# The order of twelve matmuls in a token-major weight unit: low weights first, and two PSUM banks in turn

## Chip, cores and metric

The kernel runs on one core of a Trainium2 chip. The metric is the device time of one execution in microseconds (us). The kernel before takes 2206.59 us, the median of three runs (2205.45 to 2206.94). One profiled execution gives the trace that this document reads.

## What is computed

One layer of a decoder on 256 tokens with 16 learned tokens put ahead of them, in float32, with a model width of 2048:

```python
h = concat([meta, x])                                  # 16 + 256 tokens
h = h + 0.5 * swiglu(rmsnorm(h), w_gate, w_up, w_down) # 2048 -> 5632 -> 2048
h = h + mixer(rmsnorm(h), w_in, ...)                   # two attentions, sigmoid gates, w_out
h = h + 0.5 * swiglu(rmsnorm(h), w_gate, w_up, w_down)
return h[:, 16:]
# swiglu(x) = (silu(x @ w_gate) * (x @ w_up)) @ w_down
# mixer: proj = x @ w_in gives q, k, v of 8 + 8 heads and two gates;
#        (sigmoid(g_fox) * (o_fox @ w_fox) + sigmoid(g_sb) * (o_sb @ w_sb)) @ w_out
```

Nearly all the work is the products of these activations with weight matrices of 394 MB in all (from their shapes).

## The kernel before

**Products from two parts.** TensorE multiplies in a float32 form of reduced precision, so each operand is split into a high part (the value rounded to that form) and a low part (the rest). A product is the sum of three matmuls: high by high, high by low and low by high, all summed up in one PSUM bank.

**Units and blocks.** A block is one tile of columns of a weight matrix, mostly 512 wide, with its whole contraction. It is worked through in units of 1024 columns' worth of weights per partition, which for 512 columns are two k-tiles of 128 rows. For each unit SyncE loads the raw weights (`load`), ScalarE rounds them to the high weights `wh` (L190, or L1130 in a group, see below), VectorE subtracts to get the low weights `wl` (L191 or L1136), and TensorE multiplies (`products`). There are three buffers each of `wh` and `wl` (`SPLIT_BUFS`), and a unit is split two units ahead of its products (`ahead`).

Units come in four kinds:

- feature-major units with 272 tokens (24 matmuls of 272 columns, L1204): the first feed-forward layer, keys and values;
- "wide" units with 256 tokens (L1187, L1190): queries and the output projection;
- **token-major units** (`by_token`): here the activations are the stationary operand, 128 tokens by 128 features, and the weights stream by, 512 columns. Each block has two halves of 128 tokens, and each half has a bank of its own. A unit has 2 k-tiles x 2 halves x 3 terms = 12 matmuls. 216 units in 44 blocks are of this kind: the gates (64 units), the two branch projections (32), the first two column groups of the second feed-forward layer (32) and its down projection (88). That is 2592 of the program's 13716 matmuls;
- **group units** (class `Group`, L1003): column groups 2 to 10 of the second feed-forward layer are done with seven products p1 to p7 of half size instead of eight. A group has 28 units with 6 matmuls of 512 columns each, all into one bank. Some of them read weight sums formed earlier, and the units of p2 cost VectorE one more subtraction (L1135).

In the second feed-forward layer the group units and the token-major units (second column group first, then the down projection) are interleaved: a token-major unit follows each unit of p2, every second unit of p5 and p3, and one unit each of p1 and p7, as long as there are any; the last 14 follow at the end.

**A token-major unit before.** L1181 loops over the halves j, and inside it L1192 over the k-tiles i. For each (j, i) come high activations by high weights, high activations by low weights, low activations by high weights (L1195 to L1204). So the six matmuls of half 0 come first, then the six of half 1. After each half, if the block ends there, its bank is emptied (`b.evac`, for the down projection `down2`, L933), and `tick()` is called twice.

**Lanes.** `tick()` advances small side jobs written as generators: the attention of the heads, the sigmoids of the gates, and the transposes of finished activations (`turn`, L440). A job yields the number of ticks until its next step. A group unit ticks once, a token-major unit four times.

**Order.** The program text gives each instruction a place. The order in which each engine really runs them is fixed when the program is built, by a planner with its own estimates of durations: an instruction whose inputs are not due yet by those estimates may be passed by a later one on the same engine. Matmuls into the same bank stay in the order of the text. On the chip each engine then runs its list in order.

Of the kernel before, what the change touches and what calls it, by code (L numbers as in the profile page):

```python
# [16 lines left out]
P = 128  # L17
# [35 lines left out]
def hybrid_layer(ctx: ExitStack, tc: tile.TileContext, x, meta_tokens, ffn1_norm, ffn1_w_gate, ffn1_w_up,  # L53
# [3 lines left out]
    act, dve, pe = nc.scalar, nc.vector, nc.tensor  # L57
# [21 lines left out]
    def name(tag):  # L79
        uid[0] += 1  # L80
        return f"{tag}_{uid[0]}"
# [4 lines left out]
    def temp(shape, dt, tag, bufs=1):  # L86
        return tp.tile(shape, dt, tag=tag, name=name(tag), bufs=bufs)
# [14 lines left out]
    def tick():  # L102
        for k, lane in lanes.items():
            if waits[k]:
                waits[k] -= 1
            while lane and not waits[k]:
                try:
                    waits[k] = next(lane[0]) or 1
                except StopIteration:
                    lane.pop(0)  # L110
# [863 lines left out]
    class Group:  # L974
# [18 lines left out]
        def products(self, p, u, wh, wl):  # L993
            k = self.BANK[p]
            if k not in self.banks:
                self.banks[k] = psp.tile([P, 512], F32, tag="ps", name=name("acc"))
            ps = self.banks[k]
            fresh = p in ("p1", "p2", "p4", "p5")
            xh, xl = forms[self.FORM[p]]
            for i in range(2):  # L1000
                kt = 2 * u + i
                for m, (a, b) in enumerate(((xh, wh), (xh, wl), (xl, wh))):
                    pe.matmul(ps[:], a[:, kt, :], b[:, i, :], start=fresh and kt == 0 and m == 0,  # L1003
                              stop=kt == 7 and m == 2, skip_group_check=True)
            if u == 3:
                getattr(self, p)(ps)
# [97 lines left out]
    raws, halves, banks, newest = {}, {}, {}, []  # L1104
# [63 lines left out]
    def products(u):  # L1168
        b, k0, n = units[u]
        wh, wl = halves.pop(u)  # L1170
        if isinstance(b, Group):
            b.products(k0, n, wh, wl)
            tick()
            return
        outs = 2 if b.by_token else b.cols // P
        if k0 == 0:
            if b.before:
                b.before()
            banks[b] = [psp.tile([P, 512], F32, tag="ps", name=name("acc")) for _ in range(outs)]
        wide = not b.by_token and b.n == NR  # L1180
        for j in range(outs):  # L1181
            ps = banks[b][j]
            cs = slice(j * P, (j + 1) * P)
            if wide:
                xs_of = [b.rhs(k0 + i) for i in range(n)]
                for i, x in enumerate(xs_of):
                    pe.matmul(ps[:].rearrange("p (a t) -> p a t", a=2), wh[:, i, cs], x[:, :, :NR],  # L1187
                              start=k0 + i == 0, stop=False, skip_group_check=True)
                for i, x in enumerate(xs_of):
                    pe.matmul(ps[:, :NR], wl[:, i, cs], x[:, 0, :NR], start=False, stop=k0 + i == b.kts - 1,  # L1190
                              skip_group_check=True)
            for i in range(0 if wide else n):  # L1192
                x = b.rhs(k0 + i)
                first, last = k0 + i == 0, k0 + i == b.kts - 1
                if b.by_token:  # L1195
                    xh, xl = (x[0][j], x[1][j]) if isinstance(x, list) else (x[:, 0, cs], x[:, 1, cs])
                    terms = ((ps[:], xh, wh[:, i, :]), (ps[:], xh, wl[:, i, :]), (ps[:], xl, wh[:, i, :]))
                elif b.stacked:
                    terms = tuple((ps[:, :b.n], wh[:, i, cs], x[:, m, :b.n]) for m in range(2))
                else:  # L1200
                    o, xh, xl = ps[:, :b.n], x[:, 0, :b.n], x[:, 1, :b.n]
                    terms = ((o, wh[:, i, cs], xh), (o, wh[:, i, cs], xl), (o, wl[:, i, cs], xh))
                for m, (o, a, c) in enumerate(terms):
                    pe.matmul(o, a, c, start=first and m == 0, stop=last and m == len(terms) - 1)  # L1204
            if wide and k0 + n == b.kts:
                t = temp([P, NR], F32, "sum", bufs=3)
                act.activation(t[:], ps[:, NR:2 * NR], AF.Copy)
                dve.tensor_tensor(t[:], t[:], ps[:, :NR], op=ALU.add)
                ps = t
            if k0 + n == b.kts:  # L1210
                if b is blocks[0]:
                    held.append((b.evac, j, ps))
                else:
                    b.evac(j, ps)
            for _ in range(2 if b.by_token else 1):
                tick()
        if k0 + n == b.kts:
            del banks[b]
# [42 lines left out]
    with tc.manual_schedule(engines={act.engine, dve.engine}):  # L1261
        act.preload_act_table_set(LN_EXP)
        first_start()
        first_products(0)
        first_norm(1)
        first_products(1)
        raws.pop(0)
        halves.pop(0)
        for u in range(1, KT // 2 - 1):
            first_norm(u + 1)  # L1270
            if u == KT // 2 - 3:
                lanes["misc"] += [first_factors(), first_block(), other_constants()]
            products(u)
    done = KT // 2
    start = KT // 2 - 1
    for u in range(start, len(units)):
        ahead(u)
        products(u)
# [33 lines left out]
```

## Time and profile before

| | |
|---|---|
| median of three runs | 2206.59 us (2205.45 to 2206.94) |
| the profiled execution's own time | 2207.63 us |
| its span, first to last instruction | 2205.9 us |
| granted TensorE clock, mean | 0.999 |
| TensorE busy, matmuls | 2199.1 us, 13716 instructions |
| VectorE busy | 1603.0 us |
| ScalarE busy | 1170.5 us |
| memory traffic | 250 GB/s over the span |

Rows of the groups view have: line, engine, operation, output tile <- input tiles, shape, count | busy us, mean ns of one | idle time of the engine before them, and what ended it. In this kernel `v` and `f` are buffers of activations (and of other values), `acc` is a PSUM bank of a block, `aux` one of a side job. So `acc<-wh,v` with 512 columns is a token-major matmul with high weights. Rows of the timeline have: start us, duration us, engine, line, operation, tiles, shape and how many in a row were merged; in brackets the idle time before and what ended it. PE is the matmul, PEld the load of the stationary operand, which runs ahead of its matmul. The ends of matmuls are modelled (a 512-column one always shows 0.39 us or more), so the step from one start to the next is the measure of what one costs. A start can likewise be shown early where the load of its stationary operand came late.

### The profile page before, as it was taken

Reading aid. Unit: us, or ns where it says so; the run is one execution under the profiler, and the core shown is the slowest. Engines: PE = TensorE matmul, PEld = TensorE weight load, DVE = VectorE, ACT = ScalarE, POOL = GpSimd, SP = SyncE. Lnnn points to the kernel's source line nnn. Section 1 sums busy time; section 2 is a strip of 40 time slices with the busy share of each in tenths; the row PEclk is TensorE's granted clock in tenths of the full one; section 3 lists DMA queues with packets and bytes.
Section 4 is the critical chain, followed back from the end, with each engine's and each line's share of the span. In section 5 each row is a group of like instructions: output and inputs, shape, how many; then the busy total and the mean of one; then the engine's idle time right before and its main releaser. Section 6 shows DMA issues by size and latency. Waiting matters only on the chain.

```text
span 2205.9 us, 34841 instructions
## 1 busy us (share of the span) xinstructions
PE 2199.1 (100%) x13716; PEld 1997.0 (91%) x13716; DVE 1603.0 (73%) x1944; ACT 1170.5 (53%) x1467; POOL 42.1 (2%) x113
## 2 busy tenths in 40 slices
PE   9999999999999999999999999999999999999999
PEld 9999999999999999998899988888888888888887
DVE  6676666667766765889556665667888888888886
ACT  6344433334443454656445565458666666666663
POOL 0000000000000001110000000000000000000000
PEclk9999999999999999999999999999999999999999
DMA  7899999999999966555655456555788777888774
GB/s 225 281 330 324 340 318 348 343 338 333 347 336 340 323 202 191 164 166 158 190 183 164 146 156 201 179 187 163 241 272 269 261 262 260 275 272 270 258 260 171
DMA packets 262021, 554.09 MB, mean 251 GB/s; under 512 B 17289, under 2 KB 22241, under 8 KB 261857
## 3 DMA queue, kind: packets, MB, share of 16 engines
q1 hardware_dynamic: 259776, 548.34, 75.2%
q8 instruction: 107, 1.75, 0.3%
q10 hardware_dynamic: 1472, 2.37, 0.3%
q0 software_dynamic: 608, 1.16, 0.2%
q14 instruction: 58, 0.47, 0.1%
HBM read 493.07 MB, written 58.73 MB: 250 GB/s over the span
## 4 chain that ended last, share of the span: by engine, by line
PE 99%; DMA 0%; DVE 0%; SPq 0%; issue 0%; DVEq 0%; ACT 0%
PE acc L1204 72%; PE acc L1003 16%; PE acc L1187 5%; PE acc L1190 3%; PE aux L727 1%; PE aux L600 1%; PE aux L440 1%; PE aux L588 0%; PE aux L698 0%; DMA v<-in_meta_tokens_dram 0%; PE acc L1165 0%; PE aux L866 0%; PE aux L340 0%; PE aux L677 0%; PE aux L678 0%; PE aux L640 0%
## 5 line engine op out<-in xcount | busy, mean ns | idle before, releaser
L190 ACT ACTIVATE wh<-raw 128x1024 fp32r<-128x1024 f32 (+1 forms) x609 | 644.4, 1059 | 779.1 <-PE acc L1204 621.9
L191 DVE TENSOR_TENSOR wl<-raw,wh 128x1024 fp32r<-128x1024 f32 (+1 forms) x609 | 743.1, 1222 | 432.3 <-ACT wh L190 428.3
L1204 PE MATMUL acc<-v,wh 128*128 128x272 f32 x5264 | 991.4, 288 | 0.0
L1204 PEld LDWEIGHTS acc<-v,wh 128*128 128x128 f32 x5264 | 827.4, 189 | 0.1
L1204 PE MATMUL acc<-v,wl 128*128 128x272 f32 x2616 | 753.5, 289 | 0.4 <-DVE wl L191 0.4
L1204 PE MATMUL acc<-wh,v 128*128 128x512 f32 x1664 | 540.8, 392 | 0.0
L1204 PEld LDWEIGHTS acc<-v,wl 128*128 128x128 f32 x2616 | 490.8, 188 | 0.8 <-DVE wl L191 0.6
L1204 PEld LDWEIGHTS acc<-wh,v 128*128 128x128 f32 x1664 | 312.5, 188 | 64.6
L1136 DVE TENSOR_TENSOR wl<-raw,wh 128x1024 fp32r<-128x1024 f32 x252 | 305.1, 1221 | 41.5 <-ACT wh L1130 33.4
L1130 ACT ACTIVATE wh<-raw 128x1024 fp32r<-128x1024 f32 x252 | 266.5, 1060 | 124.3 <-PE acc L1204 75.4
L1204 PE MATMUL acc<-wl,v 128*128 128x512 f32 x832 | 327.8, 394 | 0.0
L1204 PEld LDWEIGHTS acc<-wl,v 128*128 128x128 f32 x832 | 156.2, 188 | 38.8 <-DVE wl L191 7.1
L1003 PE MATMUL acc<-wh,f 128*128 128x512 f32 x576 | 191.3, 393 | 0.0
L1187 PE MATMUL acc<-v,wh 128*128 128x512 f32 x512 | 160.6, 395 | 0.0
L1003 PE MATMUL acc<-wh,v 128*128 128x512 f32 x432 | 143.3, 389 | 0.0
L1003 PEld LDWEIGHTS acc<-wh,f 128*128 128x128 f32 x576 | 108.2, 188 | 22.5
L1190 PEld LDWEIGHTS acc<-v,wl 128*128 128x128 f32 x512 | 96.1, 188 | 22.0
L1003 PE MATMUL acc<-wl,f 128*128 128x512 f32 x288 | 113.2, 393 | 0.0
L1190 PE MATMUL acc<-v,wl 128*128 128x256 f32 x512 | 101.3, 279 | 0.0
L1003 PEld LDWEIGHTS acc<-wh,v 128*128 128x128 f32 x432 | 81.1, 188 | 16.9
L1003 PE MATMUL acc<-wl,v 128*128 128x512 f32 x216 | 84.0, 389 | 0.0
L1187 PEld LDWEIGHTS acc<-v,wh 128*128 128x128 f32 x512 | 78.4, 188 | 0.2
(264 smaller groups left out, 1378.5 us busy)
## 6 DMA issues: line engine op xcount, KB each, us to landing
raw<-in_ffn_w_down_dram SPq DMA_DIRECT2D x176, 512.0 KB, 5.4
raw<-in_ffn_w_gate_dram SPq DMA_DIRECT2D x175, 512.0 KB, 5.2
raw<-in_w_in_dram SPq DMA_DIRECT2D x162, 512.0 KB, 3.7
raw<-in_ffn_w_up_dram SPq DMA_DIRECT2D x140, 512.0 KB, 5.1
sum<-pre SPq DMA_DIRECT2D x108, 512.0 KB, 6.5
raw<-sum SPq DMA_DIRECT2D x108, 512.0 KB, 4.6
pre<-in_ffn_w_up_dram SPq DMA_DIRECT2D x72, 512.0 KB, 6.9
pre<-in_ffn_w_gate_dram SPq DMA_DIRECT2D x36, 512.0 KB, 6.8
```

The lines of the kernel that those rows point to most:

```text
L190: act.activation(hi, src, AF.Copy)
L191: dve.tensor_tensor(lo, src, hi.bitcast(F32), op=ALU.subtract)
L440: pe.transpose(p[:, (2 * j + i) * P:(2 * j + i + 1) * P], u[:, i, c:c + P], ident[:])
L600: pe.matmul(po[:, :NR], a[:, ks], b[:, i * NR:(i + 1) * NR], start=n == 0, stop=n == 6)
L727: pe.matmul(o, a, b, start=start, stop=stop, skip_group_check=True)
L1003: pe.matmul(ps[:], a[:, kt, :], b[:, i, :], start=fresh and kt == 0 and m == 0, stop=kt == 7 and m == 2, skip_group_check=True)
L1130: act.activation(wh[:], raw[:], AF.Copy)
L1136: dve.tensor_tensor(wl[:], raw[:], wh[:].bitcast(F32), op=ALU.subtract)
L1187: pe.matmul(ps[:].rearrange("p (a t) -> p a t", a=2), wh[:, i, cs], x[:, :, :NR], start=k0 + i == 0, stop=False, skip_group_check=True)
L1190: pe.matmul(ps[:, :NR], wl[:, i, cs], x[:, 0, :NR], start=False, stop=k0 + i == b.kts - 1, skip_group_check=True)
L1204: pe.matmul(o, a, c, start=first and m == 0, stop=last and m == len(terms) - 1)
```

## The change

In a token-major unit all twelve matmuls are now issued ahead of the loop over halves. For each of the two k-tiles i they are: high activations by **low** weights for half 0 and half 1, then high activations by high weights for both halves, then low activations by high weights for both. So successive matmuls go to the two banks in turn, and the first two of a unit read the low weights. The emptying of the banks and the ticks stay in the loop over halves, with the same order among themselves, and so come behind all twelve. Number, shapes and operands of the matmuls are the same; in each bank the order of the three terms differs.

```diff
+        if b.by_token:
+            todo = [(i, l, m, j) for i in range(n) for l, m in ((1, 0), (0, 0), (0, 1)) for j in range(outs)]
+            for i, l, m, j in todo:
+                x = b.rhs(k0 + i)
+                a = x[m][j] if isinstance(x, list) else x[:, m, j * P:(j + 1) * P]
+                pe.matmul(banks[b][j][:], a, (wh, wl)[l][:, i, :], start=k0 + i + m == 0 and l == 1,
+                          stop=k0 + i == b.kts - 1 and m == 1)
         for j in range(outs):
             ps = banks[b][j]
...
-            for i in range(0 if wide else n):
+            for i in range(0 if wide or b.by_token else n):
                 x = b.rhs(k0 + i)
                 first, last = k0 + i == 0, k0 + i == b.kts - 1
-                if b.by_token:
-                    xh, xl = (x[0][j], x[1][j]) if isinstance(x, list) else (x[:, 0, cs], x[:, 1, cs])
-                    terms = ((ps[:], xh, wh[:, i, :]), (ps[:], xh, wl[:, i, :]), (ps[:], xl, wh[:, i, :]))
-                elif b.stacked:
+                if b.stacked:
                     terms = tuple((ps[:, :b.n], wh[:, i, cs], x[:, m, :b.n]) for m in range(2))
```

## The prediction

> **What bounds the kernel now.** I read the page first: the busy times and the chain that ended last; then who TensorE's loads waited for; then the timeline at those places.
>
> ```profile
> span 2205.9 us, 34841 instructions
> PE 2199.1 (100%) x13716; PEld 1997.0 (91%) x13716; DVE 1603.0 (73%) x1944; ACT 1170.5 (53%) x1467; POOL 42.1 (2%) x113
> PE 99%; DMA 0%; DVE 0%; SPq 0%; issue 0%; DVEq 0%; ACT 0%
> ...
> PEld acc L1204 <- DVE wl L191: 9.4, 29, 0.6
> PEld acc L1003 <- DVE wl L1136: 1.3, 7, 0.2
> ```
>
> TensorE is the chain from end to end. A change of order can move the end in two ways only: through the step from one matmul to the next, or through idle time of TensorE. The only waits that recur in the steady part are those of the last two rows, and both are for low weights. That is what the change touches: it makes a unit ask for its low weights with its first matmul, not its second.
>
> **The step.** Near the end of the trace there are token-major units alone, with nothing late:
>
> ```profile
> 2200.17 0.39 PE L1204 MATMUL acc<-wl,v 128*128 128x512 f32 x1
> 2200.39 0.62 PE L1204 MATMUL acc<-wh,v 128*128 128x512 f32 x2
> ...
> 2200.82 0.75 DVE L933 SCALAR_TENSOR_TENSOR v<-acc,v 128x256 f32<-128x256 f32 x2 [3.23 <-PE acc L1204]
> ...
> 2201.76 0.39 PE L1204 MATMUL acc<-wh,v 128*128 128x512 f32 x1
> ...
> 2202.18 0.76 DVE L933 SCALAR_TENSOR_TENSOR v<-acc,v 128x256 f32<-128x256 f32 x2 [0.60 <-PE acc L1204]
> ...
> L933 DVE SCALAR_TENSOR_TENSOR v<-acc,v x50: 414/682/692, 1708.2 to 2202.5; 128x512 f32<-128x512 f32 x46, 128x256 f32<-128x256 f32 x4
> ```
>
> The last row gives one piece of the emptying by itself (shortest, median, longest in ns). From 2200.17 to 2201.76 are seven steps: 0.227 us each, in one bank but for one. Does a change of bank make it shorter? The side jobs have a place where two banks take turns (L640 and L641) and others of the same widths in one bank:
>
> ```profile
> 969.84 0.29 PE L640 MATMUL aux<-kqh,onesr 128*128 128x272 f32 x1
> ...
> 970.33 0.39 PE L1204 MATMUL acc<-wh,v 128*128 128x512 f32 x1
> ...
> 974.47 0.40 PE L600 MATMUL aux<-R,vh 128*128 128x256 f32 x2
> ...
> 975.30 0.40 PE L1204 MATMUL acc<-wh,v 128*128 128x512 f32 x1
> ...
> 1040.71 0.29 PE L677 MATMUL aux<-kqh 128*128 128x272 f32 x1
> ...
> 1041.08 0.40 PE L1204 MATMUL acc<-wh,v 128*128 128x512 f32 x1
> ```
>
> In turn: two of 272 and two of 256 columns take 0.49 us. In one bank: seven of 256 take 0.83 (0.119 each), three of 272 take 0.37 (0.123 each), so two and two would take 0.484. The turn gains nothing that the trace can tell. The same number of matmuls at the same step: 0.
>
> **Where low weights are late.** Three kinds of place, all in the interleaved part of the second feed-forward layer. Kind A, at 1744:
>
> ```profile
> 1743.03 1.05 ACT L1130 ACTIVATE wh<-raw 128x1024 fp32r<-128x1024 f32 x1
> 1743.17 1.23 DVE L191 TENSOR_TENSOR wl<-raw,wh 128x1024 fp32r<-128x1024 f32 x1 [0.57 <-ACT wh L190]
> ...
> 1744.11 0.39 PE L1204 MATMUL acc<-wh,v 128*128 128x512 f32 x1
> 1744.45 0.50 PE L1204 MATMUL acc<-wl,v 128*128 128x512 f32 x1
> 1744.79 0.64 PE L1204 MATMUL acc<-wh,v 128*128 128x512 f32 x2
> ```
>
> The unit starts at 1744.11, its low weights are finished at 1744.40. The next matmul but one starts at 1744.79, so the one with low weights really ran from 1744.79 - 0.227 = 1744.56: 0.17 after the end of the subtraction, 0.45 after the unit's start. Of that, 0.227 is covered by the first matmul; TensorE idles 0.23. Kind B, at 1763:
>
> ```profile
> 1763.44 0.62 PE L1204 MATMUL acc<-wh,v 128*128 128x512 f32 x2
> 1763.89 0.27 PE L440 MATMUL aux<-ident,v 128*128 128x128 f32 x1
> 1763.92 0.48 PE L1003 MATMUL acc<-wh,f 128*128 128x512 f32 x1
> 1764.26 0.50 PE L1204 MATMUL acc<-wl,v 128*128 128x512 f32 x1
> 1764.60 0.62 PE L1204 MATMUL acc<-wh,v 128*128 128x512 f32 x2
> ```
>
> Here the planner knew that the low weights would be late and filled: the first matmul of half 0, the first of half 1 (another bank, so it may pass), a transpose, the first matmul of the next group unit. The low weights could be used from 1764.60 - 0.227 = 1764.37, 0.93 after the start. Kind C, at 1990:
>
> ```profile
> 1987.45 1.28 DVE L933 SCALAR_TENSOR_TENSOR v<-acc,v 128x512 f32<-128x512 f32 x2
> 1988.65 1.21 DVE L1135 TENSOR_TENSOR raw<-raw,raw 128x1024 f32<-128x1024 f32 x1
> ...
> 1990.23 0.61 PE L1003 MATMUL acc<-wh,f 128*128 128x512 f32 x2
> 1990.68 0.62 PE L1204 MATMUL acc<-wh,v 128*128 128x512 f32 x2
> ...
> 1990.92 1.22 DVE L191 TENSOR_TENSOR wl<-raw,wh 128x1024 fp32r<-128x1024 f32 x1
> 1991.13 0.42 PE L1003 MATMUL acc<-wl,f 128*128 128x512 f32 x1
> 1991.39 0.62 PE L1003 MATMUL acc<-wh,f 128*128 128x512 f32 x2
> ...
> 1992.31 0.40 PE L1204 MATMUL acc<-wl,v 128*128 128x512 f32 x1
> ```
>
> Now a **group** unit lacks its low weights, and the two leading matmuls of the next token-major unit, which need high weights alone, are put in front of it. They fill 0.45 us; the group unit's low weights are usable from 1991.39 - 0.227 = 1991.16, 0.03 after that.
>
> The count comes from the two rows of waits: 7 of L1003 are kind C (first at 1668, last at 2125). Of the 29 of L1204, following the timeline, one is in a feature-major unit at 320 and one in a token-major unit at 1542; 8 are kind B (1629 to 2099) and 19 kind A (1571 to 2147). One more filled place without a wait is at 1561.
>
> **The change, costed.** Low weights first means that a token-major unit has nothing to offer before they are there: both banks begin with them, and in a bank the order holds. Those leading high matmuls were the cover.
>
> - Kind C: the group unit's low weights come when they came (1991.16), the two matmuls in front of it are gone: 0.45 us idle at each, 7 x 0.45 = 3.2. After that follow five group matmuls to 1992.30, and the token-major low weights (finished 1990.92 + 1.22 = 1992.14, plus 0.17) are there at 1992.31: nothing further.
> - Kind B: of four fills the transpose and the group matmul stay; 0.45 us each goes. 8 x 0.45 = 3.6; at best, with three more transposes of 0.11 put in, 8 x 0.12 = 1.0.
> - Kind A: 0.227 us of cover goes; without a fill 19 x 0.227 = 4.3. With the fill it is nothing: the high weights of the next group unit are finished at 1743.03 + 1.05 = 1744.08, before 1744.11, and its first matmul needs only them. Will the planner put it there? In kind B it still filled at 0.56 and no longer at 0.79, while the chip had the weights at 0.93: its estimates run 0.14 to 0.37 early. In kind A the chip has them at 0.45, so the planner expects them at 0.08 to 0.31 after the start, and then it fills. I take 0; end for the range 4.3.
> - The single places at 1542 and 1561: 0.23 and 0.45, together 0.7.
> - Other token-major units of that part, 56 of them, stand as the one at 1749:
>
> ```profile
> 1748.41 1.23 DVE L191 TENSOR_TENSOR wl<-raw,wh 128x1024 fp32r<-128x1024 f32 x1 [0.40 <-ACT wh L190]
> ...
> 1749.84 0.39 PE L1204 MATMUL acc<-wh,v 128*128 128x512 f32 x1
> ```
>
> Finished at 1749.64, usable at 1749.81, start at 1749.84: on time by 0.03. I take 0; with 0.05 each it would be 2.8. This margin is tight but it is tied: the high weights wait for the buffer of the unit three back, whose last reader is in both orders a unit's twelfth matmul. The low buffer comes free at the eighth instead of the eleventh, but the subtraction waits for the high weights anyway: no gain. In the gates, the branches and at the end no row of waits names a token-major unit: 0.
>
> - Emptying: half 0 was emptied under the six matmuls of half 1; now both halves come together, at the end. Down-projection rows show 1.28 us for two. The next block writes other banks of the eight, so TensorE doesn't wait; VectorE does both (0.6 apart) in the 1.3 us before the next high weights are rounded. At kind C VectorE goes from the emptying at 1987.45 without a gap to the late low weights, and half 0's would now wait for the unit's end at about 1987.7: 0.26 each if nothing is put in front, 7 x 0.26 = 1.8. I take 0, since the subtraction of L1135, next in its list, needs no matmul.
> - The very end has no such cover (one piece takes 0.42, two 0.76): the last matmul is at 2201.76, VectorE starts 0.42 later at 2202.18. Now half 0's two pieces begin at 2201.53 + 0.42 = 2201.95 and take two steps of 0.34, so half 1's begin at 2202.63: +0.45.
> - Ticks: four at the end of a unit, where there were two and two. The number and what they issue are the same; a job that feeds TensorE yields 4 to 7 ticks before it goes on, at least one unit of 2.7 us, and what isn't due the planner passes. 0, at most 1.
>
> Sum: 3.2 + 3.6 + 0 + 0.7 + 0.45 = **7.9 us**. Against the profiled execution's 2207.63 that is 2215.5; the profiled execution is 1.0 above the median, so I forecast 2206.6 + 7.9 = **2214.5 us**.
>
> **Rivals.**
> 1. *The cover only moves (no change).* The planner finds other fills at B and C as it did with the transpose: then B costs its lower bound 1.0, C half of its 3.2, and with the single places and the end it is 1.0 + 1.6 + 0.7 + 0.45 = 3.7: 2210.3. For it: it does fill. Against: at C the next unit's high weights aren't ready yet and nothing else is in sight. 0.28.
> 2. *Faster: the turn of banks shortens the step.* The place is the 2592 token-major matmuls; each ns is worth 2.6 us, and from 1.7 ns the kernel is measurably faster. If the step fell to 0.220, the time would be 2206.6 + 7.9 - 18 = 2196. Against it are the rows of the turn above; for it only that 0.227 is more than 512 columns need at the rate of the steps between 256 and 512 (0.227 - 0.119 = 0.108 per 256), a fixed 0.011 that has some cause. 0.12.
>    The Trainium skill, "TensorE: Matmul & The Clock Gate", section "Wait — 56ns, not 53.3ns?", gives 215.7 ns from start to start at 512 columns; the trace shows 227, and by the page's figure 29 us would lie in these units if the bank were the cause. The page doesn't say so.
> 3. *Slower than forecast.* No fill at A (4.3), VectorE's late emptying (1.8), the tight 56 (2.8): up to +17, 2223. For it: the planner left A unfilled before. 0.1.
> 4. *Much slower: each block loses an overlap.* If emptying half 0 under half 1 was cover everywhere, each of the 44 blocks loses the 0.6 us of one half: 26 us more, 2233 from the median alone. Against it: the emptying at 1987.45 ran on while TensorE went on to a group unit in another bank. 0.02.
>    The Trainium skill has such a rule, which speaks against this change: in "Perfetto Trace Analysis", section Matmuls, independent matmul groups should rotate through different banks so that emptying one overlaps the next one's matmuls. By that rule the 26 us would stand; the trace bears it out for the last block only.
> 5. *The change does nothing,* because the planner restores the old order. It can't: within a bank the text holds. Under 0.01.
>
> **How the numbers follow.** Forecast 0.48 with a range of its own of 2211 to 2219; rivals 0.28, 0.12, 0.1, 0.02 and next to nothing. A difference under 0.2% (4.4 us: 2202.2 to 2211.0) can't be told from no change in this kernel. Slower: forecast and rivals 3 and 4, 0.6. No change: rival 1, 0.28. Faster: 0.12. The range 2204 to 2221 takes in rival 1 and the upper ends of most terms.
>
> **What will show it.** Right: the waits of L1204's successor for `wl` of L191 grow from 9.4 us, those of the group line from 1.3 us by some 3; at kind C no token-major pair stands in the group unit; at kind A a group matmul stands ahead of the first low one; the token-major step is still 0.227. Wrong: a step of 0.225 or less; waits unchanged (then planner fills); or new waits of ScalarE or side jobs, which I cost at nothing.

## The result, and the profile after

| | before | after |
|---|---|---|
| median | 2206.66 us (five runs, 2205.45 to 2207.09) | 2219.88 us (five runs, 2219.06 to 2222.62) |
| ratio | 1 | 1.0063, 95% interval 1.0052 to 1.0075 |
| the profiled execution: its time, its span | 2207.63, 2205.9 us | 2221.49, 2219.8 us |
| last matmul's start to the end of the span | 4.17 us | 4.70 us |

The change makes the kernel slower by 13.2 us between the medians, 0.60% (the ratio in the table is that of the means). The forecast was 7.9 us, so the direction was right and the size too small: the median lies 0.9 us above the forecast's own range of 2211 to 2219 and inside the wide one of 2204 to 2221. In the kernel after, L1186 is the token-major line (L1204 before); L1003 is still the group line.

Three rows of the page of the kernel after, then its waits of TensorE's loads (us in total, times, longest):

```profile
span 2219.8 us, 34842 instructions
PE 2207.2 (99%) x13716; PEld 1994.6 (90%) x13716; DVE 1603.1 (72%) x1944; ACT 1168.3 (53%) x1467; POOL 41.4 (2%) x113
PE 96%; ACT 2%; DVE 2%; issue 1%; DMA 0%; SPq 0%; DVEq 0%; ACTq 0%
...
PEld acc L1186 <- DVE wl L191: 11.5, 27, 0.7
PEld acc L1003 <- ACT wh L1130: 7.3, 23, 0.8
PEld acc L1003 <- DVE wl L1136: 5.6, 9, 0.8
```

The same matmuls, but the chain that ended last now leaves TensorE for 3 to 4% of the span, to the two engines that make the weights. The second row of waits is new: group loads that wait for **high** weights. All 23 are group matmuls that the planner pulls forward: 19 at kind A, three at kind B, one at 1561. Most of this wait is the load's alone; the table below counts what it costs the matmuls.

Where is it? Busy time by stage of the kernel after (window | its length, PE busy and instructions, PEld, DVE, ...):

```profile
960.00:1558.00 598.00, 597.75 (x3378) 523.48 (x3377) 402.11 (x568) 336.80 (x467) 17.22 (x49) 1.00 0.57 174
1700.00:1900.00 200.00, 198.76 (x866) 158.84 (x867) 167.44 (x157) 127.14 (x134) 0.00 (x0) 1.00 0.79 260
1900.00:2166.00 266.00, 263.54 (x1148) 209.82 (x1147) 225.67 (x214) 171.43 (x181) 0.00 (x0) 1.00 0.78 260
```

And of the kernel before:

```profile
960.00:1558.00 598.00, 597.92 (x3377) 523.39 (x3376) 401.87 (x568) 338.47 (x467) 18.12 (x49) 1.00 0.57 174
1700.00:1900.00 200.00, 200.00 (x884) 162.75 (x883) 171.41 (x163) 131.38 (x138) 0.00 (x0) 1.00 0.80 267
1900.00:2166.00 266.00, 266.00 (x1176) 216.39 (x1176) 231.14 (x221) 174.02 (x183) 0.00 (x0) 1.00 0.80 266
```

In the gates, attention and branches nothing changes: 3378 matmuls against 3377. In the last of these windows TensorE starts 1148 instructions instead of 1176, at 0.227 us some 6 us less work in the same time. The granted clock is 1.00 in all. So all of the loss lies where group units and token-major units alternate.

To place it there, each step from one matmul's start to the next was compared with its nominal one (0.227 us at 512 columns, 0.108 for a transpose) and the excess added up. From 1558 to 2166 that is 7.3 us before and 20.6 after, +13.3. With +0.53 behind the last matmul this is 13.8, and the spans differ by 13.9. By kind of place:

| place | count | before, us | after, us | difference | predicted |
|---|---|---|---|---|---|
| C, in a group unit | 7 | 0.1 | 4.2 (0.60 each) | +4.1 | +3.2 |
| B | 8 | 1.1 (0.14 each) | 4.6 (0.49, three times 0.71) | +3.4 | +3.6 |
| A | 19 | 4.2 (0.22 each) | 5.0 (0.16 to 0.33, once 0.70) | +0.8 | 0 |
| D, the next token-major unit after a kind A | 18 | 0 | 3.4 (0.19 each) | **+3.4** | **0** |
| the place at 1561 | 1 | 0 | 0.4 | +0.4 | +0.45 |
| steps with under 0.08 too much | many | 1.9 | 3.1 | +1.2 | 0 |

A step counts as such a place from 0.08 us of excess; smaller ones, such as the 0.03 at six of the seven kind C places before, stand in the last row. The place at 1542 gives another 0.3, and between 1250 and 1450 the excess is 0.4 smaller, without a kind of place that repeats.

**Kind C, in the kernel after.** The timeline at 2000:

```profile
1999.21 1.22 DVE L1136 TENSOR_TENSOR wl<-raw,wh 128x1024 fp32r<-128x1024 f32 x1
...
1999.54 0.61 PE L1003 MATMUL acc<-wh,f 128*128 128x512 f32 x2
...
2000.48 0.50 PE L1003 MATMUL acc<-wl,f 128*128 128x512 f32 x1 [0.33 <-DVE wl L1136]
...
2000.81 0.62 PE L1003 MATMUL acc<-wh,f 128*128 128x512 f32 x2
```

No token-major pair stands in front of the late matmul. It is due at 1999.54 + 2 x 0.227 = 1999.99 and really runs from 2000.81 - 0.227 = 2000.58, 0.59 late. (The bracket says 0.33, because the ends of matmuls are modelled and this start is shown early.)

**Kind B,** at 1767:

```profile
1766.65 1.22 DVE L191 TENSOR_TENSOR wl<-raw,wh 128x1024 fp32r<-128x1024 f32 x1
1766.87 0.39 PE L1003 MATMUL acc<-wh,f 128*128 128x512 f32 x1
...
1767.10 0.27 PE L440 MATMUL aux<-ident,v 128*128 128x128 f32 x1
...
1767.13 0.48 PE L1003 MATMUL acc<-wh,f 128*128 128x512 f32 x1
...
1767.45 0.27 PE L440 MATMUL aux<-ident,v 128*128 128x128 f32 x1
...
1768.48 1.09 PE L1186 MATMUL acc<-wh,v 128*128 128x512 f32 x4
```

The unit's turn comes at 1766.87 + 0.227 = 1767.10. The low weights can be used from 1768.48 - 2 x 0.227 = 1768.03, 0.93 later, exactly as before. The transpose and the group matmul still fill, one more transpose was found (0.11), and the 0.45 of the two high matmuls is gone: 0.48 idle.

**Kinds A and D,** the same kind of unit at 1747 and the next one at 1753:

```profile
1746.65 1.23 DVE L191 TENSOR_TENSOR wl<-raw,wh 128x1024 fp32r<-128x1024 f32 x1 [0.57 <-ACT wh L190]
...
1747.36 0.75 PE L1003 MATMUL acc<-wh,v 128*128 128x512 f32 x2
...
1747.95 0.71 PE L1186 MATMUL acc<-wl,v 128*128 128x512 f32 x2
...
1748.50 0.85 PE L1186 MATMUL acc<-wh,v 128*128 128x512 f32 x3
...
1750.97 1.06 ACT L190 ACTIVATE wh<-raw 128x1024 fp32r<-128x1024 f32 x1 [2.12 <-PE acc L1186]
...
1752.07 1.22 DVE L191 TENSOR_TENSOR wl<-raw,wh 128x1024 fp32r<-128x1024 f32 x1
...
1753.04 0.39 PE L1003 MATMUL acc<-wh,v 128*128 128x512 f32 x1
...
1753.35 0.73 PE L1186 MATMUL acc<-wl,v 128*128 128x512 f32 x2
...
1753.92 0.62 PE L1186 MATMUL acc<-wh,v 128*128 128x512 f32 x2
```

At A the planner does what was predicted: the second of the two matmuls shown at 1747.36 belongs to the next group unit. It takes the place of the high matmul, and the idle time stays at 0.2. But then the unit at 1753 is late. Its subtraction starts at 1752.07 and its turn comes at 1753.04 + 0.227 = 1753.27: 1.20 us. In the prediction's rows of 1748 the subtraction starts at 1748.41 and the turn comes at 1749.84: 1.43 us. The missing 0.23 is one matmul. The rounding of those weights (1750.97) starts when the unit of kind A has ended and its buffer is free; up to the next token-major unit there used to be twelve group matmuls, and one of the twelve has been used up as the fill. The margin of 0.03 of the "56 tight units" becomes 0.19 too little at each of these 18.

### The profile page after: what moved, and what is told of

Its sections match the earlier page's. It is cut to its first block, busy times and chain, and to the rows that moved or that the text cites. A ratio compares the mean times of both kernels' runs of the same rounds, so it can differ in the third digit from the quotient of the medians.

```text
span 2219.8 us, 34842 instructions
## 1 busy us (share of the span) xinstructions
PE 2207.2 (99%) x13716; PEld 1994.6 (90%) x13716; DVE 1603.1 (72%) x1944; ACT 1168.3 (53%) x1467; POOL 41.4 (2%) x113
## 4 chain that ended last, share of the span: by engine, by line
PE 96%; ACT 2%; DVE 2%; issue 1%; DMA 0%; SPq 0%; DVEq 0%; ACTq 0%
PE acc L1208 45%; PE acc L1186 26%; PE acc L1003 14%; PE acc L1194 5%; PE acc L1197 3%; PE aux L727 1%; PE aux L600 1%; PE aux L440 1%; DVE wl L1136 0%; DVE wl L191 0%; ACT wh L1130 0%; ACT wh L190 0%; ACT v L878 0%; DMA v<-in_meta_tokens_dram 0%; DVE v L1033 0%
## 5 line engine op out<-in xcount | busy, mean ns | idle before, releaser
L1186 PE MATMUL acc<-wh,v 128*128 128x512 f32 x1664 | 456.0, 391 | 0.0
L1186 PEld LDWEIGHTS acc<-wh,v 128*128 128x128 f32 x1664 | 312.3, 188 | 68.9
L1136 DVE TENSOR_TENSOR wl<-raw,wh 128x1024 fp32r<-128x1024 f32 x252 | 305.1, 1222 | 47.5 <-ACT wh L1130 41.8
L1186 PE MATMUL acc<-wl,v 128*128 128x512 f32 x832 | 266.1, 398 | 2.1 <-DVE wl L191 2.1
L1003 PE MATMUL acc<-wh,f 128*128 128x512 f32 x576 | 190.4, 395 | 0.0
L1186 PEld LDWEIGHTS acc<-wl,v 128*128 128x128 f32 x832 | 149.4, 188 | 39.6 <-DVE wl L191 9.9
L1003 PE MATMUL acc<-wh,v 128*128 128x512 f32 x432 | 143.1, 392 | 0.3 <-ACT wh L1130 0.3
L1003 PEld LDWEIGHTS acc<-wh,f 128*128 128x128 f32 x576 | 108.1, 188 | 25.8 <-ACT wh L1130 4.0
L1003 PE MATMUL acc<-wl,f 128*128 128x512 f32 x288 | 113.9, 396 | 2.3 <-DVE wl L1136 2.3
L1197 PEld LDWEIGHTS acc<-v,wl 128*128 128x128 f32 x512 | 96.1, 188 | 22.0
L1197 PE MATMUL acc<-v,wl 128*128 128x256 f32 x512 | 101.3, 279 | 0.0
L1003 PEld LDWEIGHTS acc<-wh,v 128*128 128x128 f32 x432 | 81.1, 188 | 19.8 <-ACT wh L1130 3.3
L1003 PE MATMUL acc<-wl,v 128*128 128x512 f32 x216 | 84.1, 390 | 0.0
```

What stands on the lines that cost most here:

```text
L1136: dve.tensor_tensor(wl[:], raw[:], wh[:].bitcast(F32), op=ALU.subtract)
L1186: pe.matmul(banks[b][j][:], a, (wh, wl)[l][:, i, :], start=k0 + i + m == 0 and l == 1, stop=k0 + i == b.kts - 1 and m == 1)
```

## The experiments

Each was measured against the kernel before on the same chip: median 2206.61 us for the first four, 2206.21 for the last two.

**1. High matmuls first, everything else as in the change.** For each k-tile high by high of both halves, then high by low, then low by high. The flags that open and close a bank's sum move with the order, here and in the next runs; of such lines the cuts below show only a part, or none.

```diff
-  for l, m in ((1, 0), (0, 0), (0, 1)) for j in range(outs)]
+  for l, m in ((0, 0), (1, 0), (0, 1)) for j in range(outs)]
```

> The changed kernel with only its first two terms exchanged: per k-tile high by high for both halves, then high activations by low weights, then low by high. Banks in turn and emptying at the end stay. Theory 'low first' (the loss is the cover that the leading high matmuls gave): two leading high matmuls cover 0.45 us, so kind A falls from 0.22 to about 0 at its 19 places, B and C are as in the kernel before, the end costs 0.5: about 2203 us, no group unit waits for high weights. Rival 'turn of banks' (the joint emptying and the turn cost the time): it stays above 2212 us.

Measured: 2203.36 us, ratio 0.9985 (0.9976 to 0.9994), 16.5 us below the changed kernel. The waits of TensorE's loads in this kernel:

```profile
PEld acc L1003 <- DVE wl L1136: 2.1, 7, 0.3
PEld acc L1186 <- DVE wl L191: 2.0, 10, 0.4
```

The banks still take turns and both are still emptied together, yet the loss is gone, and more. Two leading matmuls cover 0.45 instead of the 0.23 of the kernel before, so kind A (0.45 late) has no idle time but at one place, and D has gone with the fills. B is back at 0.14 each. It is the low weights' place in the order that costs, not the turn of the banks.

**2. All eight high matmuls of a unit first, the four low ones last.** The banks still take turns.

```diff
-  todo = [(i, l, m, j) for i in range(n) for l, m in ((1, 0), (0, 0), (0, 1)) for j in range(outs)]
+  todo = [(i, l, m, j) for l, m in ((0, 0), (0, 1), (1, 0)) for i in range(n) for j in range(outs)]
```

> All eight matmuls of a unit with high weights first, both halves in turn, then the four with low weights. Theory 'low first': eight leading matmuls cover 1.8 us, which is over the 0.93 of kind B, and the buffer of high weights comes free at the eighth instead of the twelfth matmul, so that the split three units on may start 0.9 us earlier: the stalls of A, B and C all go, 7 us less than the kernel before and 0.5 more at the end: about 2200 us. Rival: the low weights' buffer, now free only at the twelfth, becomes the bound and VectorE's subtraction waits for TensorE: no better than 2203 us.

Measured: 2202.05 us, ratio 0.9979 (0.9970 to 0.9988), 2 us more than expected. The waits, and kind C in this kernel:

```profile
PEld acc L1003 <- DVE wl L1136: 2.1, 7, 0.3
...
1986.05 0.61 PE L1186 MATMUL acc<-wh,v 128*128 128x512 f32 x2
...
1986.89 0.62 PE L1003 MATMUL acc<-wh,f 128*128 128x512 f32 x2
```

No token-major unit waits any more in the interleaved part; the excess there is 1.3 us instead of 20.6. Kind C keeps 0.15 at each of its seven places, 1.1 of the 2 us (from 1986.05 to 1986.89 it is 0.84, where two token-major matmuls and the late group matmul are due in 0.68). Its fill is back, two token-major matmuls as before the change, where 0.03 was left at six of the seven. From the last matmul to the end it is 4.71 us, as after the change. What are the 0.12 more at kind C? The next run tells.

**3. Low weights first, but the halves one after the other as before the change.** No turn of banks, each half emptied and ticked by itself:

```diff
 # the loops of the kernel before; inside a half:
-  terms = ((ps[:], xh, wh[:, i, :]), (ps[:], xh, wl[:, i, :]), (ps[:], xl, wh[:, i, :]))
+  terms = ((ps[:], xh, wl[:, i, :]), (ps[:], xh, wh[:, i, :]), (ps[:], xl, wh[:, i, :]))
```

> Low weights first, but one half after the other as in the kernel before: banks not in turn, half 0 emptied under half 1, two ticks after each. Theory 'low first': as slow as the changed kernel but for the end, 2218 to 2219.5 us, with the same waits for low weights. Rival 'turn of banks': near the kernel before plus the one matmul of cover at kind A, about 2209 us. Kind C tells how much of its 0.60 us per place is the late emptying: 0.45 here if the rest was that.

Measured: 2219.33 us, ratio 1.0060 (1.0047 to 1.0074). That is 12.7 us more than before, so nearly all of the 13.2 us comes from the low weights' place alone. A, B and D are as after the change; from the last matmul to the end it is 4.17 us again. Kind C is a little better, 0.47 instead of 0.60. The group matmul in this run, and the VectorE work that leads to its weights:

```profile
1992.35 2.55 DVE L1136 TENSOR_TENSOR wl<-raw,wh 128x1024 fp32r<-128x1024 f32 x2 [0.18 <-ACT wh L1130]
1994.82 1.28 DVE L933 SCALAR_TENSOR_TENSOR v<-acc,v 128x512 f32<-128x512 f32 x2
1996.02 1.21 DVE L1135 TENSOR_TENSOR raw<-raw,raw 128x1024 f32<-128x1024 f32 x1
1997.15 1.22 DVE L1136 TENSOR_TENSOR wl<-raw,wh 128x1024 fp32r<-128x1024 f32 x1
...
1998.42 0.50 PE L1003 MATMUL acc<-wl,f 128*128 128x512 f32 x1 [0.20 <-DVE wl L1136]
```

The same stretch of VectorE in the kernel after the change:

```profile
1994.29 2.54 DVE L1136 TENSOR_TENSOR wl<-raw,wh 128x1024 fp32r<-128x1024 f32 x2 [0.19 <-ACT wh L1130]
1996.87 1.22 DVE L1135 TENSOR_TENSOR raw<-raw,raw 128x1024 f32<-128x1024 f32 x1
1998.01 1.28 DVE L933 SCALAR_TENSOR_TENSOR v<-acc,v 128x512 f32<-128x512 f32 x2
```

With halves, the emptying (L933) comes first and the added subtraction of p2 (L1135) behind it. With both halves together, the planner puts L1135 in front. That was the prediction's reason to cost the late emptying at nothing, and the size is nearly right: the 0.26 at each place doesn't come. But from the first row to the late subtraction it is 1999.21 - 1994.29 = 4.92 us instead of 1997.15 - 1992.35 = 4.80. All of it lies at one handover: L933 is shown starting 0.08 before the pair of L1136 ends, L1135 0.04 after. Why, the trace doesn't say. The same stretch, wherever it occurs (six times in each trace), takes 4.91 or 4.92 in the kernel after and in runs 1 and 2, which empty both halves together, and 4.78 to 4.80 in the kernel before and in runs 3 and 5, which don't. Since VectorE is the late one here, kind C pays 0.12 for it, in run 2 too.

**4. The change, but the planner may not let matmuls of the second feed-forward layer pass one another.** Each unit's matmuls are kept behind the last one of the unit before:

```diff
+  with tc.issue_after(before[-1]) if before else ExitStack():
+      q = pe.matmul(banks[b][j][:], a, (wh, wl)[l][:, i, :], ...)
...
+  if u >= second:
+      before.append(q.ins)
```

The group units' matmuls get the same. The lines move with the edit: L1190 is the token-major line here, L1004 the group line.

> The changed kernel, with the matmuls of each unit of the second feed-forward layer kept behind the last one of the unit before, so that no group matmul can be put ahead of a late token-major unit. Theory 'borrowed': the 0.19 us stalls that follow each kind A two or three units later come from that very fill (the units in between have one matmul fewer left to cover the split): they vanish (18 x 0.19 = 3.4 less), A grows to 0.45 each (3.6 more), B to 0.71 each (1.1 more): 2220 to 2222 us. Rival 'the fill is a gain, the 0.19 are late by themselves': 4.7 us more and they stay: about 2224.6 us.

Measured: 2223.65 us (2221.86 to 2228.0, four runs), ratio 1.0082 (1.0068 to 1.0095): between the two expectations, and its interval overlaps that of the change. The trace tells more: between 1558 and 2166 the excess is 23.1 us, 2.4 more than after the change and not 4.7. (The profiled execution is the fastest of the four, and 2.0 us ahead within its first 12 us; its span is therefore only 0.4 longer than that of the change.) The same two units as above:

```profile
1746.13 0.39 PE L1004 MATMUL acc<-wh,v 128*128 128x512 f32 x1
1746.70 0.73 PE L1190 MATMUL acc<-wl,v 128*128 128x512 f32 x2 [0.18 <-DVE wl L191]
1747.27 1.09 PE L1190 MATMUL acc<-wh,v 128*128 128x512 f32 x4
...
1750.87 1.22 DVE L191 TENSOR_TENSOR wl<-raw,wh 128x1024 fp32r<-128x1024 f32 x1
...
1752.06 0.39 PE L1004 MATMUL acc<-wh,v 128*128 128x512 f32 x1
1752.29 0.63 PE L1190 MATMUL acc<-wl,v 128*128 128x512 f32 x2
1752.76 1.07 PE L1190 MATMUL acc<-wh,v 128*128 128x512 f32 x4
```

Without the fill, kind A idles 0.46 here instead of 0.20 (1747.27 - 0.454 against 1746.13 + 0.227); over the 19 places it is 0.42 to 0.58, once 0.70. The next unit's subtraction starts at 1750.87 and its turn comes at 1752.06 + 0.227 = 1752.29: 1.42 us again, and it is on time. All 18 stalls of kind D are gone. So **the fill at A was borrowed**: A and D together cost 8.4 us with fills and 9.4 without, where 19 fills of 0.227 would be worth 4.3 if they were a gain. At B it is different: the eight places cost 6.3 without the group matmul and 4.6 with it, 0.22 each, and no new late place appears behind them.

**5. Half by half as before the change, but in each half the four high matmuls first, the two low ones last.**

```diff
+  for l, m in ((0, 0), (0, 1), (1, 0)):
+      for i in range(n):
+          ...
+          pe.matmul(ps[:], a, (wh, wl)[l][:, i, :], start=k0 + i + m + l == 0,
+                    stop=k0 + i == b.kts - 1 and l == 1)
```

> Edit: token-major units half by half again, as before the change, but inside a half the four matmuls with high weights of both k-tiles come first, then the two with low weights. The emptying of half 0 lies under half 1 again. Theory (the time hangs on when the low weights are asked for, and the emptying of both halves together costs only what lies at the very end): four leading matmuls cover 4 x 0.227 = 0.91 us, which kinds A and B need (0.45 and 0.93), so their stalls go as in the run with all eight high matmuls first; kind C keeps about 0.11 x 7 = 0.8; from the last matmul to the end of the span it is 4.2 us again instead of 4.7. Against that run's 2202.05 median this gives 2200.8 to 2201.6. Rival (the emptying together cost nothing, or the buffer of the high weights, which now comes free at the unit's tenth matmul instead of its eighth, brings the stalls at the rounding back): 2202 or more, with waits of the token-major line for low weights above 3 us in all.

Measured: 2201.04 us, ratio 0.9976 (0.9967 to 0.9985), as the theory expected. The end is 4.17 us again. Kind B in this kernel (L1197 is its token-major line), and its waits:

```profile
1760.63 1.22 DVE L191 TENSOR_TENSOR wl<-raw,wh 128x1024 fp32r<-128x1024 f32 x1
...
1761.08 1.07 PE L1197 MATMUL acc<-wh,v 128*128 128x512 f32 x4
...
1762.47 1.09 PE L1197 MATMUL acc<-wh,v 128*128 128x512 f32 x4
...
PEld acc L1197 <- DVE wl L191: 1.4, 8, 0.2
...
PEld acc L1003 <- DVE wl L1136: 1.3, 7, 0.2
```

Six steps from 1761.08 to 1762.47 take 1.39 where 6 x 0.227 = 1.36 are due: the low weights, 0.94 after the unit's turn, cost 0.03. One thing in the expectation failed: kind C was to keep 0.8 us in all. It has the waits of the kernel before (1.3 in 7) and 0.03 each. The 0.12 more in run 2 was the joint emptying, and the theory had not connected the two.

**6. Run 5, and the group units too take their high weights first.**

```diff
-  for i in range(2):
-      kt = 2 * u + i
-      for m, (a, b) in enumerate(((xh, wh), (xh, wl), (xl, wh))):
+  for m, (a, b) in enumerate(((xh, wh), (xl, wh), (xh, wl))):
+      for i in range(2):
+          kt = 2 * u + i
```

> Edit: the run before this one, and the group units of the second feed-forward layer too take their four high-weight matmuls first and the two with low weights last. Theory (a late low operand costs what is not covered by the matmuls ahead of it): a group unit has four instead of one ahead, 0.91 instead of 0.23 us, so the last recurring stalls, kind C with 7 x 0.11 = 0.8 us, go: 2200.0 to 2200.9, and the group line has under 0.3 us of waits for low weights. Rival (nothing that is late is left in these units, or the change of order makes the planner fill less and the gain comes back as another wait): the same time as the run before it within 0.3 us.

Measured: 2199.56 us, ratio 0.9972 (0.9962 to 0.9983), 0.4 below the expected range. In the interleaved part the excess goes from 1.0 to 0.1 us: nothing waits there any more. The rest of the 1.5 us between the two medians isn't explained by it. The two profiled executions differ by another 1.2 us ahead of 960, nearly all of it in the first feed-forward layer between 204 and 320: there loads of feature-major units wait for late low weights, 1.0 us in three places in run 5 and 0.2 in one in run 6. Such a wait of 0.6 at 320 is in the trace before and not in the one after the change, and no edit here touches those units, so this is no part of the gain that is shown.

## Why the prediction was right, and where not

**The bound and the step: right.** TensorE's chain is the kernel, and only idle time of TensorE moved. The step did not change with the turn of banks. From the timeline near the end of the kernel after:

```profile
2212.59 0.61 PE L1186 MATMUL acc<-wl,v 128*128 128x512 f32 x2
...
2213.95 0.61 PE L1186 MATMUL acc<-wl,v 128*128 128x512 f32 x2
...
2214.40 1.07 PE L1186 MATMUL acc<-wh,v 128*128 128x512 f32 x4
2215.28 1.41 DVE L933 SCALAR_TENSOR_TENSOR v<-acc,v 128x256 f32<-128x256 f32 x4 [4.15 <-PE acc L1186]
```

Six steps, each in the other bank, from 2212.59 to 2213.95: 0.227. Rival 2 falls, and the 215.7 ns that the Trainium skill gives ("TensorE: Matmul & The Clock Gate", section "Wait — 56ns, not 53.3ns?") are not reached by taking the banks in turn.

**Kind B: right** (+3.4 against 3.6). The high matmuls' 0.45 went. At five of the eight places the group matmul and the transpose stayed and a second transpose was found, a step towards the lower bound with its three more; at the other three (1835, 1973, 2110) the group matmul stands alone and 0.93 - 0.227 = 0.71 are idle. The two kinds of miss nearly cancel.

**Kind C: mechanism right, 0.9 too small.** The pair of 0.45 was gone as foreseen. Of the rest, 0.12 x 7 = 0.8 is the joint emptying that was taken at 0 with an upper end of 1.8 (run 3).

**Kind A and the 56 tight units: the step that failed.** "With the fill it is nothing" was read at the place itself, and there it holds within 0.8 us. But the fill was one of the twelve matmuls that lie between the release of the weight buffers and their next use, and the prediction had both facts in hand: the loop over the buffers ("This margin is tight but it is tied") and the margin of 0.03. It argued that the margin does not move with the order inside a unit, and did not ask whether the fill takes work out of the loop. 18 x 0.19 = 3.4 us of the 6.0 us missing in the forecast, counted between the spans, are this; C's 0.9, A's 0.8 and the 1.2 us of small steps are the rest, less the 0.4 between 1250 and 1450. The upper ends named for these terms (4.3 and 2.8) would have covered it, but for other reasons: no fill at A, and all 56 units late by 0.05. That the wide range of the forecast held is in this part luck.

**The very end: right.** 0.53 against 0.45 us. The four pieces start at 2215.28, 0.42 after half 0's last matmul at 2214.86, and take 1.41.

**The rivals.** "The cover only moves" (rival 1) falls: at B one more transpose came at five places, at C no fill at all, and the fills that did come at A were paid back later. "Slower than forecast" (rival 3, given 0.1) is where the time came out: of its three terms the late emptying came at 0.8 of 1.8, the unfilled A not at all, and the tight units at 3.4, but at 18 of them and because of the fills. The emptying as cover of every block (rival 4, 26 us) falls: runs 1 and 2 empty both halves together in all 44 blocks and are faster than the kernel before. The rule of the Trainium skill behind it, "Perfetto Trace Analysis", section Matmuls, asks that independent groups of matmuls take different banks in turn, so that emptying one overlaps the next one's matmuls. The blocks do that in all these kernels, and emptying the halves together cost 1.3 us in all (0.5 at the end, 0.12 at each kind C). New waits of ScalarE were named as a sign against; they came (7.3 us of loads), because the fills wait for their high weights. At kind A that happens in time in which the low weights are late anyway. Whether these waits account for the small steps isn't settled.

**What the change was worth.** Its two parts, separated: low weights first costs 12.7 us (run 3); the turn of banks with the joint emptying costs about 0.5 us between the medians of the change and run 3, and 0.6 between runs 2 and 5 (4.6 and 5.2 us gained on the kernel before; they differ in how many high matmuls lead as well), against 1.3 us counted at its places. The opposite order, with the late operand last, gains 5.2 us on the kernel before (run 5), and 6.7 with the group units (run 6), which is the fastest kernel here.

## What to carry to other kernels

Where several terms are summed in one bank, ask first for the operand that is ready first. Every matmul that can run ahead of a late operand is cover, and how much is needed is read as the time from the unit's turn to the late operand (here 0.45 and 0.93 us, so two and four matmuls of 0.227). When a planner fills a stall, look where the filling work was taken from: if it lay between the release of a buffer and its next use, the stall comes back there.

## What the runs showed of the hardware beside that

- Taking two PSUM banks in turn instead of staying in one made no difference to the step of 512-column matmuls: 0.227 us in both.
- Low weights could be used 0.15 to 0.18 us after the end of their subtraction, whatever the kind of unit: 0.15 in the rows of kind C (1999.21 + 1.22 = 2000.43, used from 2000.58), 0.16 in B, 0.17 in A, 0.18 in D (1753.29, used from 1753.92 - 0.454 = 1753.47).
- On VectorE the same five instructions (L1136 twice, L933 twice, L1135) took 0.12 us longer with L1135 ahead of L933 than behind it, through one handover (run 3).
